# A two-layer hybrid trunk on one core: bias rows from one stacked tile, a third step ahead of the transposes, and the end of the last quad after the first output product

## The chip, the cores and the metric

The kernel runs on one core of one Trainium2 chip. Its time is device microseconds (us) of that core. Three runs of the kernel before took 1513.29 to 1514.67 us, with a median of 1514.11. The engines are named as in the profile: PE (TensorE matmuls), PEld (its weight loads), DVE (VectorE), ACT (ScalarE), POOL (GpSimd), SP (which issues the DMAs).

## The reference

The input has 512 positions of width 1024; 16 learned meta positions are put in front, so that 528 are computed. Layer 0 mixes by two kinds of attention side by side, layer 1 by retention; each is followed by a residual with layer norm and by an MLP with squared ReLU (1024 to 4096 to 1024), a residual and a layer norm. What the change touches:

```python
proj = h @ w_in                      # qa, ka, va | qb, kb, vb | fb
log_f = log_sigmoid(fb + f_bias)     # 8 heads of forgetting attention
cum_f = cumsum(log_f, axis=1)        # along the positions
# differential attention: 4 heads, two softmaxes each, chunk mask
p_diff = p_a[:, :, 0] - lam * p_a[:, :, 1]
# forgetting attention: 8 heads, causal
s_b = (qb . kb) * scale_b + cum_f[q] - cum_f[k]
o_b = softmax(where(frame_vis, s_b, -inf)) @ vb
# MLP
y = square(relu(h @ w1)) @ w2
```

## The kernel before

Positions lie along the free axis: an activation is eight tiles of 128 features by 528 positions, worked on as two halves of 264. Products run in fp32r, with each operand split into a high and a low part; a product is three matmuls (high by high, high by low, low by high). The high part of a weight tile is cast by ACT (`wh`, L228), the low part comes from DVE (`wl`, L229). Activations are split in the same way (`s`, L352 to L362). All matmuls go through one helper (L156) and all transposes on PE through another (L159), so that rows of the profile with those lines are told apart by their tiles.

Order: instructions are written in program order and a scheduler places them on each engine's queue. For PE the written order is fixed. Pieces of work that do not depend on each other are interleaved by Python generators: a filler yields after each piece, and the attention code calls `next(filler, None)` where PE would otherwise run ahead of ACT and DVE. One piece of a projection is 12 matmuls of 264 columns (`mm`). PSUM is shared: `two_banks` tiles (`mm`, `rows_ps` and the like) come from a ring of two, so that a new one needs the older one's reader to have finished.

Layer 0, in the order of time. The value projection (`v_ps`, 512 columns) comes first. Then the four differential heads run: scores (`s_ps`), a clip with its minimum on DVE (L548), exponentials on ACT (L554), normalization on DVE and ACT (L621 to L625), transposes on PE (`t_ps`, 14 of them), their conversion (`turned`, L583 on ACT and L584 on DVE; `s`, L352 and L353), and the products with the values (`o_ps`). Between them the projections of the next heads run as filler.

During the second differential head the filler also builds the bias of the forgetting heads. `forget_sums` (L489 to L511) makes the cumulative sum of log-forget, 8 rows of 528, and splits it. `forget_rows` (L513 to L530) spreads it over tables: for each pair of heads g and each side (query, key) a tile of 128 rows by 528, whose rows 64 (h % 2) to 64 (h % 2) + 3 hold the sum with its sign in two parts, or ones, so that a matmul of two such tables adds cum_f[q] - cum_f[k] to the scores. A constant selection matrix `sel` (8 rows by 3 x 1024) puts each row in its place: three matmuls of 8 contraction rows for each half of a table (high, low, ones), with PE reading `selr`, the cast of `sel`. Each table is copied to SBUF by ACT (`rows`, L527). The generator yields after both sides of a pair: four steps of two tables.

Then come the four pairs of forgetting heads (`fox_scores`, L738 to L757): four score tiles with one filler step each, one more filler step, the last normalization (`finish(3)`), the small scores of the meta positions (`sm_ps`), then the first head's transposes, a filler step, the second head's transposes, more filler steps, and the products with the values.

The MLP (L1198 on) makes the hidden units in part by Strassen-like quads (`quad_up`, L1148 to L1196): seven products on quarters, `qa` to `qd`, whose last, "22", is held back in `finish`: 12 matmuls into `qc`, an addition on DVE (`up`, L1190), relu and two squares on ACT (L1192 to L1194) and a subtraction on DVE (`g`, L1195). `between()` calls a held-back finish once. Hidden units are worked off in four groups; in the last, the output products of the first two output tiles are taken together, over the hidden tiles 0 to 5 and then over 6 and 7, which the last quad makes. The output products of the others follow in `tail`, together with the residual's layer norm (`bank`).

Of the kernel before, what the change touches and what calls it, by code (L numbers as in the profile page):

```python
# [8 lines left out]
F32 = mybir.dt.float32  # L9
F32R = mybir.dt.float32r  # L10
# [4 lines left out]
P = 128  # L15
# [5 lines left out]
HALF = L // 2  # L21
STACK = 6 * META
# [3 lines left out]
FOX_HEADS = 8  # L26
# [95 lines left out]
def kernel(  # L122
# [20 lines left out]
    act, dve = nc.scalar, nc.vector  # L143
# [16 lines left out]
    pe = Ordered()  # L160
# [13 lines left out]
    def two(dt=F32, name="u"):  # L174
        t = both(dt, name)
        return t[:, 0, :], t[:, 1, :]

    def flat(dt, name):
        return both(dt, name).rearrange("p a b -> p (a b)")[:, :1024]
# [7 lines left out]
    def two_banks(name="mm"):  # L187
        return ps_mm.tile([P, 2, 512], F32, tag="mm", name=name)
# [4 lines left out]
    def f(t):  # L193
        return t.bitcast(F32)
# [85 lines left out]
    def product(outs, pairs, lo=0, hi=None):  # L280
        hi = len(pairs) if hi is None else hi
        for k in range(lo, hi):
            lhs, rhs = pairs[k]
            for i, (a, b) in enumerate(PASSES):
                for dst, sel in outs:
                    pe.matmul(dst, lhsT=lhs[a], rhs=sel(rhs[b]), start=k == 0 and i == 0,
                              stop=k == len(pairs) - 1 and i == 2)
# [61 lines left out]
    def split(src, dst=None, rows=slice(0, P), n=L):  # L349
        src = src[:, :n]  # L350
        h, l = dst or two(F32R, "s")
        act.copy(out=h[rows, :n], in_=src)  # L352
        dve.tensor_tensor(out=l[rows, :n], in0=src, in1=f(h)[rows, :n], op=ALU.subtract)  # L353
        return h, l
# [14 lines left out]
    def load(out, in_):  # L369
        dma = nc.sync.dma_start(out=out, in_=in_)  # L370
        if loads["last"] is not None:
            after(dma, loads["last"])
        loads["last"] = dma
        return dma

    prepare(load)
    for j in range(KT // 2):
# [3 lines left out]
        for i in range(2):  # L381
# [3 lines left out]
                     in_=f(pair)[:, :, :META].rearrange("p a (o n) -> p a o n", o=1).broadcast_to([P, 2, 2, META]))  # L385
# [3 lines left out]
    lv_sb, b4_sb = two(F32, "lv_b4")  # L389
    lv_sb = lv_sb[:, :256].rearrange("p (a b) -> p a b", a=4)  # L390
    b4_sb = b4_sb[:, :512].rearrange("p (a b) -> p a b", a=4)
    sel = [flat(F32, "sel") for _ in range(3)]
    nb = two(F32, "nb") + two(F32, "nb")
    fm = two(F32, "fm")[0]
    dve.memset(ones, 1.0)
# [2 lines left out]
    def load_constants():  # L398
        for h in range(DIFF_HEADS):
            load(out=nb[h], in_=c_nb[h])  # L400
        load(out=mb_sb, in_=c_mb)
        load(out=lv_sb, in_=lamv)
        load(out=ident, in_=c_id)
        load(out=wfb_sb, in_=wfb)
        load(out=fb_sb, in_=fbias)
        for j in range(3):
            load(out=sel[j][0:FOX_HEADS], in_=c_sel[j])
        load(out=fm, in_=c_fm)
        load(out=e4_sb, in_=c_e4[:, :4 * PAIR].rearrange("p (a b) -> p a b", a=4))
        load(out=b4_sb[:PAIR], in_=c_e4[:PAIR, 4 * PAIR:].rearrange("p (a b) -> p a b", a=4))  # L410
        load(out=sub_sb, in_=subln)
        load(out=lnp_sb, in_=lnp)
# [64 lines left out]
    R8 = slice(0, FOX_HEADS)  # L477
# [11 lines left out]
    def forget_sums(ze, into):  # L489
        z, e, t, r = (v[R8] for v in ze + two(F32, "ft"))  # L490
        dve.scalar_tensor_tensor(out=e, in0=z, scalar=-1.0, in1=z, op0=ALU.mult, op1=ALU.max)
        act.activation(out=e, in_=e, func=AF.Exp, scale=-1.0)
        yield
        dve.tensor_scalar(out=t, in0=e, scalar1=1.0, scalar2=None, op0=ALU.add)
        dve.tensor_scalar(out=r, in0=t, scalar1=-1.0, scalar2=None, op0=ALU.add)
        dve.tensor_tensor(out=e, in0=e, in1=r, op=ALU.subtract)
        yield
        act.activation(out=t, in_=t, func=AF.Ln)
        act.activation(out=r, in_=t, func=AF.Exp, scale=-1.0)
        dve.tensor_tensor(out=e, in0=e, in1=r, op=ALU.mult)  # L500
        yield
        dve.tensor_tensor(out=t, in0=t, in1=e, op=ALU.add)
        dve.scalar_tensor_tensor(out=z, in0=z, scalar=0.0, in1=t, op0=ALU.min, op1=ALU.subtract)
        yield
        dve.memset(r, 1.0)
        cum = two(F32, "cum")[0][R8]
        dve.tensor_tensor_scan(out=cum, data0=r, data1=z, initial=0.0, op0=ALU.mult, op1=ALU.add)
        one = two(F32R, "one")[0]
        act.copy(out=one[R8], in_=r)
        yield  # L510
        into += [t[R8] for t in split(cum, rows=R8)] + [one[R8]]  # L511

    def forget_rows(srcs, table):  # L513
        selr = [flat(F32R, "selr") for _ in range(3)]
        for j in range(3):
            act.copy(out=selr[j][R8], in_=sel[j][R8])
        yield
        for g in range(4):
            sides = two(F32R, "rows")
            for side in range(2):  # L520
                ps = two_banks("rows_ps")
                for b in range(2):
                    for j in range(3):
                        m = (2 * g + side) * 3 + j
                        pe.matmul(ps[:, b, :HALF], lhsT=selr[m // 8][R8, P * (m % 8):P * (m % 8) + P],
                                  rhs=srcs[j][:, b * HALF:b * HALF + HALF], start=j == 0, stop=j == 2)
                act.copy(out=on(sides[side], FULL), in_=ps[:, :, :HALF])  # L527
                if side:
                    yield
            table.append(sides)  # L530

    MAPS = [slice(64 * m, 64 * m + 64) for m in range(2)]
# [205 lines left out]
    def fox_scores(pair, q, k, filler):  # L738
        pools = [two(F32, "e") for _ in range(3)]
        maps = [key_tiles([t[m] for t in pools]) for m in range(2)]  # L740
        sums = []

        def finish(i):
            for m in range(2):
                r = small([P, 1], "r")
                dve.reciprocal(out=r, in_=sums[i][m])
                dve.tensor_scalar(out=maps[m][i], in0=maps[m][i], scalar1=r, scalar2=None, op0=ALU.mult)

        for i in range(4):
            sums.append(score_tiles(q, k, i, fm, fox_rows[pair], [t[i] for t in maps]))  # L750
            if i:
                finish(i - 1)
            next(filler, None)
        next(filler, None)
        finish(3)
        meta_scores(q, k, fox_rows[pair], 8 + 2 * pair, sm_f)
        return maps  # L757
# [57 lines left out]
    for h in range(4):  # L815
        q, k = got
        got = []
        if h < 3:
            filler = qk_filler(got)
            if h == 0:  # L820
                next(filler)
            if h == 1:
                filler = alternate(filler, forget_sums(fb_ps, sums))
            if h == 2:
                filler = alternate(filler, forget_rows(sums, fox_rows))
        else:
            bw = [weights("B") for _ in range(4)]
            filler = value_filler(bw, vb)
# [369 lines left out]
    def mlp(hs, full, a, b, norm, gs, steps=LN_STEPS):  # L1198
        ts = []
        mix = combined(a, b, ts)  # L1200
        while len(gs) < 8:
            dst = two(F32R, "g")
            get, run = job(hs, squared(dst))
            run(get(), full)
            gs.append(dst)
            for _ in range(4):
                next(mix, None)
        run_all(mix)
        left = {"finish": lambda: None}

        def between():
            left["finish"]()
            left["finish"] = lambda: None

        def quads(into, n):
            for _ in range(n):
                gh, gl = both(F32R, "g"), both(F32R, "g")
                left["finish"] = quad_up(hs, ts, a, b, (gh, gl), between)
                into += [(gh[:, i, :], gl[:, i, :]) for i in range(2)]

        for g in range(NG):
            nxt = []
            if g and g + 1 < NG:
                quads(nxt, 1)
            jobs = [job(gs, add_into(y[k], ALPHA if g == 0 else None)) for k in range(KT)]
            if g + 1 == NG:
                between()
                parts = [dense_parts(weights("A"), gs, full) for _ in range(2)]
                for lo, hi in ((0, 6), (6, 8)):
                    for _, outs, pairs in parts:  # L1230
                        product(outs, pairs, lo, hi)
                for k, (ps, _, _) in enumerate(parts):
                    add_into(y[k], None)(ps, full)
                parts = ps = outs = pairs = None
                pe.on = False
                return tail(jobs[2:], full, a, b, norm, steps)
            for k, (get, run) in enumerate(jobs):
                run(get(), full)
                if k == 0:
                    between()  # L1240
                advance()
                advance()
            pe.on = True
            gs = nxt
            quads(gs, 4 - len(gs) // 2)
# [251 lines left out]
```

## Time and profile before

| what | value |
| --- | --- |
| median of three runs | 1514.11 us |
| the profiled execution | 1510.88 us |
| its span | 1509.1 us |
| PE busy | 1468.2 us, 97% |
| DVE / ACT busy | 889.0 us, 59% / 661.0 us, 44% |
| mean granted PE clock | 0.985 |
| PE waits for ACT's copy of `rows` | 4.1 us in 4 waits |
| first and last start of a `rows_ps` matmul | 92.9 and 120.8 us |

All views are of one profiled execution. A row of the timeline gives start, duration, engine, line, operation and tile, and in brackets the idle time of the engine before it with what released it. Runs of short matmuls stand in one row with their count; the duration of such a row runs to the modelled end of the last, so the spacing of the starts is the rate. A granted clock of 0.5 means that a matmul takes twice the time. The views of windows cut the span at chosen times and give each engine's busy time and the clock in each.

### The profile page before, as it was taken

The numbers are of one execution on the slowest core, as the hardware profiler recorded it, in microseconds if no ns is written. First come the engines' busy times: TensorE is split into PE (matmuls) and PEld (weight loads), VectorE is DVE, ScalarE is ACT, GpSimd is POOL, SyncE is SP. The second block draws the span as 40 slices with busy tenths as digits, with TensorE's granted clock in tenths as the row PEclk, the third lists the DMA queues.
The fourth block names the chain that finished last, engine by engine and source line by source line (L and its number), as shares of the span: only waits on it lengthen the run. The fifth ranks groups of instructions, "written<-read, shape, count | busy, mean of one in ns | idle before, by whom it ended". The sixth has DMA issues, their size and how long they took to land.

```text
span 1509.1 us, 23262 instructions
## 1 busy us (share of the span) xinstructions
PE 1468.2 (97%) x9776; PEld 1329.8 (88%) x9776; DVE 889.0 (59%) x1498; ACT 661.0 (44%) x1024; POOL 0.2 (0%) x4
## 2 busy tenths in 40 slices
PE   8998999999999999999999999999999999999996
PEld 6877888899999999999888888888899889898986
DVE  4553468677747566558534354244378748566567
ACT  4563345536426344255343343153445526444342
POOL 0000000000000000000000000000000000000000
PEclk9987999999999999999999999999999999999998
DMA  7102111240313314243014035023150313314221
GB/s 247 57 29 70 28 43 32 100 165 6 107 56 99 126 59 138 59 145 119 27 42 134 19 110 167 1 72 109 42 182 29 112 48 107 126 56 140 74 81 56
DMA packets 39592, 129.07 MB, mean 86 GB/s; under 512 B 4724, under 2 KB 7172, under 8 KB 39488
## 3 DMA queue, kind: packets, MB, share of 16 engines
q1 hardware_dynamic: 39488, 127.59, 26.3%
q8 instruction: 76, 1.25, 0.3%
q14 instruction: 28, 0.23, 0.1%
HBM read 125.48 MB, written 2.10 MB: 85 GB/s over the span
## 4 chain that ended last, share of the span: by engine, by line
PE 90%; DVE 5%; ACT 3%; DMA 1%; issue 1%; ACTq 0%; DVEq 0%
PE bank L156 35%; PE mm L156 18%; PE v_ps L156 10%; PE qc L156 7%; PE o_ps L156 5%; PE qa L156 4%; PE s_ps L156 3%; PE qb L156 2%; PE qd L156 2%; DMA raw<-in_w 1%; PE t_ps L159 1%; PE sum_ps L156 1%; DVE wl L229 1%; ACT wh L228 1%; DVE y L966 1%
## 5 line engine op out<-in xcount | busy, mean ns | idle before, releaser
L229 DVE TENSOR_TENSOR wl<-raw,wh 128x1024 fp32r<-128x1024 f32 x200 | 242.1, 1220 | 73.3 <-ACT wh L228 72.9
L228 ACT CAST wh<-raw 128x1024 fp32r<-128x1024 f32 x200 | 206.1, 1046 | 112.0 <-DMA raw<-in_w 82.4
L156 PE MATMUL bank<-g,wh 128*128 128x512 f32 (+2 forms) x800 | 201.4, 342 | 1.0 <-ACT wh L228 1.0
L156 PEld LDWEIGHTS bank<-g,wh 128*128 128x128 f32 x800 | 137.3, 188 | 20.1 <-ACT wh L228 2.1
L156 PE MATMUL bank<-hh,wh 128*128 128x512 f32 (+3 forms) x448 | 144.1, 337 | 0.0
L156 PE MATMUL bank<-hh,wl 128*128 128x512 f32 (+3 forms) x448 | 140.3, 329 | 0.0
L156 PE MATMUL bank<-g,wl 128*128 128x512 f32 (+2 forms) x400 | 136.1, 341 | 0.0
L156 PE MATMUL mm<-g,wh 128*128 128x264 f32 x832 | 135.1, 284 | 0.5 <-ACT wh L228 0.5
L156 PE MATMUL bank<-hl,wh 128*128 128x512 f32 (+3 forms) x448 | 120.5, 331 | 4.3 <-DVE hl L958 4.3
L156 PEld LDWEIGHTS mm<-g,wh 128*128 128x128 f32 x832 | 115.3, 188 | 0.7 <-ACT wh L228 0.7
L156 PE MATMUL qc<-tc,wh 128*128 128x264 f32 (+1 forms) x576 | 106.3, 283 | 3.1 <-DVE up L1186 3.1
L156 PE MATMUL mm<-s,wh 128*128 128x264 f32 x544 | 96.8, 302 | 1.2 <-DVE od L727 1.2
L156 PEld LDWEIGHTS bank<-hh,wh 128*128 128x128 f32 x448 | 84.1, 188 | 10.6 <-ACT hh L970 1.2
L156 PEld LDWEIGHTS qc<-tc,wh 128*128 128x128 f32 x576 | 88.8, 188 | 3.7 <-DVE up L1186 3.5
L156 PEld LDWEIGHTS bank<-hh,wl 128*128 128x128 f32 x448 | 84.0, 188 | 8.4
L156 PEld LDWEIGHTS mm<-s,wh 128*128 128x128 f32 x544 | 79.5, 199 | 6.8 <-issue 2.7
L156 PEld LDWEIGHTS bank<-hl,wh 128*128 128x128 f32 x448 | 72.5, 188 | 13.9 <-DVE hl L958 4.9
L156 PE MATMUL mm<-g,wl 128*128 128x264 f32 x416 | 84.6, 285 | 0.0
L156 PEld LDWEIGHTS bank<-g,wl 128*128 128x128 f32 x400 | 75.2, 188 | 9.4 <-DVE wl L229 0.2
L156 PE MATMUL qc<-tc,wl 128*128 128x264 f32 (+1 forms) x288 | 81.7, 284 | 0.0
L228 ACT CAST wh<-sums 128x1024 fp32r<-128x1024 f32 x48 | 50.2, 1046 | 62.8 <-DVE sums L242 40.5
L229 DVE TENSOR_TENSOR wl<-sums,wh 128x1024 fp32r<-128x1024 f32 x48 | 58.6, 1221 | 24.2 <-PE mm L156 10.2
(315 smaller groups left out, 3107.3 us busy)
## 6 DMA issues: line engine op xcount, KB each, us to landing
raw<-in_w SPq DMA_DIRECT2D x224, 512.0 KB, 3.8
xf<-in_x SPq DMA_DIRECT2D x8, 264.0 KB, 5.6
y<-in_x SPq DMA_DIRECT2D x8, 264.0 KB, 4.1
out<-y SPq DMA_DIRECT2D x8, 256.0 KB, 2.2
nb<-in_c_nb SPq DMA_DIRECT2D x4, 264.0 KB
rd<-in_c_rd SPq DMA_DIRECT2D x4, 256.0 KB
rd<-in_c_rm SPq DMA_DIRECT2D x4, 192.0 KB, 4.0
fm<-in_c_fm SPq DMA_DIRECT2D x1, 264.0 KB, 2.7
```

The costliest lines, as they stand in the source:

```text
L156: return self.put(nc.tensor.matmul(*a, **k))
L159: return self.put(nc.tensor.transpose(*a, **k))
L228: act.copy(out=wh, in_=raw)
L229: dve.tensor_tensor(out=wl, in0=raw, in1=f(wh), op=ALU.subtract)
L966: dve.tensor_tensor(out=t, in0=t, in1=r, op=ALU.mult)
```

## The change

Three parts.

Bias rows: the three 8-row selection tiles become one of 96 rows (high rows from 0, low rows from 32, ones from 64), and the three sources become one tile `stack` of 96 rows with the same layout. DVE fills a base tile (64 rows of 0 and 32 of 1), ACT casts it into `stack` and casts the 8 high and the 8 low rows over it. A half of a table is one matmul with 96 contraction rows in place of three with 8. The generator yields after each table: eight steps of one table.

Third step: `fox_scores` takes one more filler step ahead of `finish(3)`. Since the filler has as many pieces as before, one fewer is left for later.

Last quad: `between()` moves from ahead of the two output products of the last group to behind the first of them (the later calls find nothing to do).

```diff
-    sel = [flat(F32, "sel") for _ in range(3)]
+    sel = flat(F32, "sel")
...
-        for j in range(3):
-            load(out=sel[j][0:FOX_HEADS], in_=c_sel[j])
+        load(out=sel[:STACK], in_=c_sel)
...
-        one = two(F32R, "one")[0]
-        act.copy(out=one[R8], in_=r)
-        yield
-        into += [t[R8] for t in split(cum, rows=R8)] + [one[R8]]
+        base, stack = two(F32, "base")[0], two(F32R, "stack")[0]
+        dve.memset(base[:64], 0.0)
+        dve.memset(base[64:STACK], 1.0)
+        act.copy(out=stack[:STACK], in_=base[:STACK])
+        h, l = split(cum, rows=R8)
+        yield
+        act.copy(out=stack[R8], in_=f(h)[R8])
+        act.copy(out=stack[32:32 + FOX_HEADS], in_=f(l)[R8])
+        into.append(stack[:STACK])
...
-        selr = [flat(F32R, "selr") for _ in range(3)]
-        for j in range(3):
-            act.copy(out=selr[j][R8], in_=sel[j][R8])
+        selr = flat(F32R, "selr")[:STACK]
+        act.copy(out=selr, in_=sel[:STACK])
         yield
         for g in range(4):
             sides = two(F32R, "rows")
             for side in range(2):
                 ps = two_banks("rows_ps")
+                m = 2 * g + side
                 for b in range(2):
-                    for j in range(3):
-                        m = (2 * g + side) * 3 + j
-                        pe.matmul(ps[:, b, :HALF], lhsT=selr[m // 8][R8, P * (m % 8):P * (m % 8) + P],
-                                  rhs=srcs[j][:, b * HALF:b * HALF + HALF], start=j == 0, stop=j == 2)
+                    pe.matmul(ps[:, b, :HALF], lhsT=selr[:, P * m:P * m + P],
+                              rhs=srcs[0][:, b * HALF:b * HALF + HALF], start=True, stop=True)
                 act.copy(out=on(sides[side], FULL), in_=ps[:, :, :HALF])
-                if side:
-                    yield
+                yield
             table.append(sides)
...
             next(filler, None)
+        next(filler, None)
         next(filler, None)
         finish(3)
...
             if g + 1 == NG:
-                between()
                 parts = [dense_parts(weights("A"), gs, full) for _ in range(2)]
                 for lo, hi in ((0, 6), (6, 8)):
                     for _, outs, pairs in parts:
                         product(outs, pairs, lo, hi)
+                        between()
```

The host's constant `c_sel` is laid out to match (96 rows by 1024).

On PE, at the tables before, around the second pair of them (`o_ps` is the product of differential head 1 with the values, `mm` a projection's piece):

```order
L156 MATMUL mm<-s,wl 128x264 x2
L156 MATMUL rows_ps<-s,selr 128x264 [waits Activation_49]
L156 MATMUL rows_ps<-s,selr 128x264
L156 MATMUL rows_ps<-one,selr 128x264
L156 MATMUL rows_ps<-s,selr 128x264 x2
L156 MATMUL rows_ps<-one,selr 128x264
L156 MATMUL rows_ps<-s,selr 128x264 [waits Activation_49]
L156 MATMUL rows_ps<-s,selr 128x264
L156 MATMUL rows_ps<-one,selr 128x264
L156 MATMUL rows_ps<-s,selr 128x264 x2
L156 MATMUL rows_ps<-one,selr 128x264
L156 MATMUL s_ps<-s 128x264 [waits DVE_49]
```

In the changed kernel, from the second table to the fourth on PE:

```order
L156 MATMUL rows_ps<-stack,selr 128x264 [waits Activation_49]
L156 MATMUL rows_ps<-stack,selr 128x264
L156 MATMUL s_ps<-s 128x264 [waits DVE_49]
...
L156 MATMUL mm<-s,wl 128x264 x2
L156 MATMUL rows_ps<-stack,selr 128x264 [waits Activation_49]
L156 MATMUL rows_ps<-stack,selr 128x264
L156 MATMUL mm<-s,wh 128x264 [waits Activation_49]
L156 MATMUL mm<-s,wh 128x264 x3
L156 MATMUL mm<-s,wl 128x264 x2
L156 MATMUL mm<-s,wh 128x264 x4
L156 MATMUL mm<-s,wl 128x264 x2
L156 MATMUL rows_ps<-stack,selr 128x264 [waits DVE_49]
```

Where two tables of six matmuls stood in a row there is one of two, and the next stands behind a piece of work; the first `mm` behind the third table, the start of the K projection, now waits for ACT.

On PE, in the first pair of forgetting heads (the first four rows are one projection piece ahead of the meta scores `sm_ps`; `t_ps` are the transposes):

```order
+L156 MATMUL mm<-s,wh 128x264 x4
+L156 MATMUL mm<-s,wl 128x264 x2
+L156 MATMUL mm<-s,wh 128x264 x4
+L156 MATMUL mm<-s,wl 128x264 x2
 L156 MATMUL sm_ps<-s 16x16 x6
 L156 MATMUL sm_ps<-rows 16x16 x2
...
 L159 MATMUL t_ps<-ident,e 128x128 x10
 L159 MATMUL t_ps<-ident,e 16x128 x4
-L156 MATMUL mm<-s,wh 128x264 x4
-L156 MATMUL mm<-s,wl 128x264 x2
-L156 MATMUL mm<-s,wh 128x264 x4
-L156 MATMUL mm<-s,wl 128x264 x2
```

Twelve matmuls have moved from behind the second transposes to ahead of the meta scores; the other pairs read alike.

On PE, at the last quad of layer 0's MLP in the changed kernel (the first `qc` run is an earlier product of that quad, the second its "22"; `mm<-g` are the two output products):

```order
L156 MATMUL qc<-tc,wl 128x264
L156 MATMUL mm<-g,wh 128x264 x4
...
L156 MATMUL mm<-g,wl 128x264 x2
L156 MATMUL qc<-tc,wh 128x264 [waits DVE_49]
L156 MATMUL qc<-tc,wh 128x264
L156 MATMUL qc<-tc,wl 128x264
...
L156 MATMUL qc<-tc,wl 128x264
L156 MATMUL mm<-g,wh 128x264 [waits Activation_49]
L156 MATMUL mm<-g,wh 128x264 x3
L156 MATMUL mm<-g,wl 128x264 [waits DVE_49]
```

Before, the two `qc` runs followed each other directly, and both output products came behind them. In the changed kernel the 36 matmuls of the first output product stand between.

More of the change, by code (lines that the diff above doesn't have):

```diff
@@ L1452 @@
     c_mb[:, 8:] = np.where(mj > mi, BIG, 0.0)[:, None, :]
-    c_sel = np.zeros((FOX_HEADS, 4, 2, 3, P))
+    c_sel = np.zeros((3, 32, 4, 2, P))
     for h in range(FOX_HEADS):
         g, base = h // 2, 64 * (h % 2)
-        c_sel[h, g, 0, 0, base] = -1.0
-        c_sel[h, g, 0, 1, base + 1] = -1.0
-        c_sel[0, g, 0, 2, base + 2:base + 4] = 1.0
-        c_sel[0, g, 1, 2, base:base + 2] = 1.0
-        c_sel[h, g, 1, 0, base + 2] = 1.0
-        c_sel[h, g, 1, 1, base + 3] = 1.0
+        c_sel[0, h, g, 0, base] = -1.0
+        c_sel[1, h, g, 0, base + 1] = -1.0
+        c_sel[2, 0, g, 0, base + 2:base + 4] = 1.0
+        c_sel[2, 0, g, 1, base:base + 2] = 1.0
+        c_sel[0, h, g, 1, base + 2] = 1.0
+        c_sel[1, h, g, 1, base + 3] = 1.0
     c_e4 = np.zeros((P, 4 * PAIR + 4 * P))
@@ L1481 @@
         "c_mb": c_mb.astype(f32),
-        "c_sel": c_sel.reshape(FOX_HEADS, 3, 1024).transpose(1, 0, 2).astype(f32),
+        "c_sel": c_sel.reshape(STACK, 1024).astype(f32),
         "c_e4": c_e4.astype(f32),
```

## The prediction

> **What bounds the kernel now.** I read the page's busy times and slices first, then its chain of waits.
>
> ```profile
> PE 1468.2 (97%) x9776; PEld 1329.8 (88%) x9776; DVE 889.0 (59%) x1498; ACT 661.0 (44%) x1024; POOL 0.2 (0%) x4
> ...
> PEclk9987999999999999999999999999999999999998
> ...
> PE 90%; DVE 5%; ACT 3%; DMA 1%; issue 1%; ACTq 0%; DVEq 0%
> ```
>
> TensorE (PE) is busy for 97% of the span and carries 90% of the chain. A change can gain only where PE idles, does needless work, or runs at a reduced clock; the clock row dips in the third and fourth slice (75 to 151 us), where the bias tables are built. Next, what PE waited for (total, times, longest):
>
> ```profile
> PE rows_ps L156 <- ACT rows L527: 4.1, 4, 1.9
> PE v_ps L156 <- DVE s L353: 3.2, 1, 3.2
> PE qc L156 <- DVE up L1186: 3.1, 2, 1.6
> PE t_ps L159 <- DVE s L362: 2.6, 2, 1.9
> PE bank L156 <- ACT wh L228: 1.0, 3, 0.6
> PE t_ps L159 <- DVE e L747: 0.7, 1, 0.7
> PE t_ps L159 <- DVE turned L584: 0.6, 2, 0.3
> PE mm L156 <- ACT wh L228: 0.5, 1, 0.5
> ```
>
> The first row is the tables' own wait, the t_ps rows lie in the forgetting attention's turns, the qc and wh rows around the MLP's last quad. Each part of the change aims at one of these groups. Last, the stretch of the tables, cut where the granted clock changed (in each row: window, its length, busy time and count of PE, PEld, DVE, ACT, POOL, then the clock):
>
> ```profile
> 94.34:97.75 3.41, 1.93 (x11) 1.66 (x12) 0.37 (x1) 2.35 (x7) 0.00 (x0) 1.00 0.30 118
> 97.75:104.60 6.85, 6.85 (x27) 5.51 (x26) 1.35 (x7) 1.97 (x6) 0.00 (x0) 0.50 0.00 0
> 104.60:108.00 3.40, 2.71 (x21) 2.22 (x21) 0.50 (x1) 1.17 (x3) 0.00 (x0) 1.00 0.00 0
> 108.00:111.35 3.35, 3.35 (x22) 3.11 (x19) 1.92 (x12) 2.00 (x6) 0.00 (x0) 0.50 0.00 0
> 111.35:114.60 3.25, 2.46 (x17) 1.96 (x16) 2.48 (x7) 3.11 (x6) 0.00 (x0) 0.99 0.00 0
> 114.60:125.00 10.40, 9.71 (x41) 8.93 (x42) 1.09 (x1) 1.77 (x3) 0.00 (x0) 0.51 0.18 52
> ...
> 230.55:234.10 3.55, 3.04 (x15) 2.74 (x15) 3.43 (x10) 1.63 (x4) 0.00 (x0) 0.55 0.19 18
> ```
>
> Each time PE idles 0.7 to 1.5 us of a window of about 3.4 us here, the next window runs at half clock. (Not without exception: PE was 0.76 us idle in
>
> ```profile
> 254.40:257.90 3.50, 2.74 (x24) 2.24 (x20) 3.50 (x13) 1.73 (x3) 0.00 (x0) 1.00 0.01 2
> ```
>
> and stayed at full rate after it.) That makes 6.85 + 3.35 + 10.40 = 20.6 us at half clock between 97.75 and 125; half of it, 10.3 us, is lost, less 0.3 for the idle time inside. I take 10.0. This is more than the waits themselves.
>
> **Part 1, the bias rows.**
>
> ```profile
> L156 PE MATMUL rows_ps<-s,selr x32: 276/286/584, 92.9 to 120.5; 8*128 8x264 f32 x32
> L156 PE MATMUL rows_ps<-one,selr x16: 273/278/420, 93.3 to 120.8; 8*128 8x264 f32 x16
> L527 ACT CAST rows<-rows_ps x8: 571/598/601, 95.2 to 121.2; 128x528 fp32r<-128x528 f32 x8
> ```
>
> 48 matmuls become 16. The pitch comes from two rows of PE's timeline, six full-clock matmuls apart and of the same 264 columns:
>
> ```profile
> 656.21 0.65 PE L156 MATMUL mm<-g,wh 128*128 128x264 f32 x4
> ...
> 656.94 0.65 PE L156 MATMUL mm<-g,wh 128*128 128x264 f32 x4
> ```
>
> 0.73 / 6 = 0.122 us each, so 32 removed are worth 3.9 us. One table per step removes the cause of the 4.1 us wait: two tables in a row share PSUM banks with the projection, so that the second had to await the copy (0.6 us) of the one before. It gains 4.1. With both gone I expect the half clock to go too: 10.0. The wait at the end of the stretch stays,
>
> ```profile
> 133.02 1.22 PE L156 MATMUL v_ps<-wh,s 128*128 128x512 f32 x2 [3.17 <-DVE s L353]
> ```
>
> since the transposes' conversion on VectorE follows directly; a stretch with less VectorE work left over might shorten it to 2.8, so 0.4. Gains at full clock: 3.9 + 4.1 + 10.0 + 0.4 = 18.4.
>
> Against this stand new waits. The stack is built ahead of the first table: two memsets on VectorE, the cast of a 96x528 base, and two 8x528 casts on ScalarE in place of one; of the three selr casts two go:
>
> ```profile
> 77.76 0.50 DVE L505 MEMSET ft<- 8x528 f32 x1
> ...
> 91.34 2.93 ACT L516 CAST selr<-sel 8x1024 fp32r<-8x1024 f32 x3
> ```
>
> Two memsets at 0.5 (528 columns as well) and a cast at 0.6 by the rows copy make 1.6 us. They sit in the queues of VectorE and ScalarE before the last exponent products (e, 128x528) of differential head 1, whose transposes PE already awaits:
>
> ```profile
> 87.14 1.42 PE L159 MATMUL t_ps<-ident,e 128*128 128x128 f32 x11 [0.53 <-DVE e L625]
> ```
>
> All of it goes on the path, and its scores behind then wait for the conversion another 0.75 by my walk through the new order. The removed 1.95 us of selr casts come too late to repay this, since by then PE waits for scores, not for selr. The bounds: 0 (the adds stay hidden) and 3.4 (they show twice). Further on, the third table (the order puts it ahead of the K projection's first matmul, which waits for its copy) is copied only after two exponents and a projection copy on ScalarE. The walk puts the table's end at about 103 and the copy's at 104.95, 1.95 us of wait; bounds 0 and 3. The last two tables still stand in a row, and the eighth waits for the seventh's copy: 0.95 us with its latency, as 0.69 and 0.79 in the old pairs; bounds 0.6 and 1.2. The load of 393 KB where three of 32 KB were lies near 35 us, with no PE wait on it between 40 and 70: nothing.
>
> Sum at full clock: 18.4 - 1.6 - 0.75 - 1.95 - 0.95 = 13.2 us. The 1.95 us wait is of the size that cost the clock before (1.48 us idle in 94.34:97.75). One such window costs half of 3.4, 1.7 us; at a chance of three in four I take 1.3 off: 11.9.
>
> The Trainium skill, page "TensorE: Matmul & The Clock Gate", Part 1, says that the gate knows only half and full rate, looks at free-running windows of about 3.4 us, falls after a window that was idle, and returns after about 3.4 us of sustained work. The trace agrees on half and full and on the grid. It disagrees on the rest: a window with PE busy 2.71 of 3.40 us was followed by half rate, and 6.85 us of unbroken work passed before full rate came back. By the page's rule no drop follows the new 1.95 us wait, and the sum would be 13.2 here and 1492.9 in all; I go by the rows.
>
> **Part 2, the third step.** Twelve matmuls, 1.46 us, move from behind the second turn to ahead of the first transposes, in four pairs of heads.
>
> ```profile
> 199.95 1.75 PE L159 MATMUL t_ps<-ident,e 128*128 128x128 f32 x14 [0.69 <-DVE s L362]
> ...
> 203.40 1.75 PE L159 MATMUL t_ps<-ident,e 128*128 128x128 f32 x14 [0.24 <-DVE turned L584]
> ...
> 231.06 3.25 PE L159 MATMUL t_ps<-ident,e 128*128 128x128 f32 x14 [1.92 <-DVE s L362]
> ...
> 288.12 1.09 PE L159 MATMUL t_ps<-ident,e 128*128 128x128 f32 x8 [0.65 <-DVE e L747]
> ```
>
> Pair 0 gains 0.69 and pair 3 0.65. Pair 1 gains 1.46 of its 1.92 and, since only 0.46 us of idle remains in that window, probably the half clock behind it (1.7, of which about 0.5 returns as a turned wait like pair 0's 0.24, which the half clock had hidden; I count 0.8). Pair 2 has no wait ahead of its first transposes and gains nothing. Sum 3.6; bounds 2.8 (the clock stays) and 4.9 (also the turned waits go). What lost its cover is the attention product behind the second turn: twelve matmuls fewer stand ahead of it. Its first half needs the first turn's tiles, which are long done, so I cost that at nothing; if it did wait, 1 us per pair.
>
> **Part 3, the last quad.**
>
> ```profile
> 654.65 0.51 PE L156 MATMUL qc<-tc,wh 128*128 128x264 f32 x2 [1.53 <-DVE up L1186]
> ...
> 661.25 0.75 PE L156 MATMUL mm<-g,wh 128*128 128x264 f32 x4 [0.47 <-ACT wh L228]
> ...
> 662.20 0.51 PE L156 MATMUL bank<-g,wh 128*128 128x264 f32 x2 [0.20 <-ACT wh L228]
> ```
>
> The quad's last twelve products wait until VectorE has emptied their bank, and the next weights' casts stand on ScalarE behind the quad's square. With one output product (36 matmuls, 4.4 us) moved between, the bank is long empty, and the new order has the three weight casts ahead of the relu. Gained: 1.53 + 0.47 + 0.20 = 2.2 in layer 0, and by the waits above (3.1 and 1.0 + 0.5 in all) 2.4 in layer 1: 4.6. The quad's result g is late next: from the last qc matmul to its end pass 656.3 to
>
> ```profile
> 660.30 1.26 DVE L1195 TENSOR_TENSOR g<-up,g 128x1056 fp32r<-128x1056 f32 x1 [3.46 <-ACT up L1194]
> ```
>
> 661.56, 5.3 us, and only the last quarter of the products reads it. The second product (4.4 us) and some two dozen bank matmuls (2.9 us) stand ahead of that: covered by 2 us. I take 4.4 for both; bounds 0 (g's chain is stretched by the casts on VectorE) and 4.6.
>
> **The sum**: 11.9 + 3.6 + 4.4 = 19.9 us. The profiled execution took 1510.88 us around a span of 1509.1, so 1491.0; it lay 3.2 us under the median of the runs, which gives 1494.2, forecast **1494**.
>
> **Rivals.** (1) The half clock stays: PE still idles in three places of the stretch, and if as much time as before (20.6 us) runs slow, 10.3 are lost instead of 1.3; gain 10.9, time 1503. For it speaks that every window there with 0.69 us of idle or more led to a slow one; against, that fewer such windows are left. (2) Neither new table wait appears (1.95 + 0.95), nor the clock drop: gain 24.1, and with all turns covered 25.4, time 1489. For it: ScalarE is busy for only 12.4 of the 30.7 us of the six windows from 94.34 on; against: the copies' order is fixed. (3) The quad's move swaps one wait for another: g arrives late and part 3 is worth nothing; 1498.6. For it, the 5.3 us of latency; against, 7.3 us of cover. (4) Slower: the clock falls at the new waits near 88 us and is not regained until the value products at 138. The full-clock gain of all parts is 13.2 + 3.6 + 4.4 = 21.2 us, and each microsecond at half rate costs 0.5, so this decides from 42 us of half clock. From 88 to 138 there are 50 us: 25 lost, 3.8 slower, 1518. For it, 97.75 to 125 held only two short full-rate windows; against, that the clock did return there while PE still idled, and with 20.6 us. By the return rule of the Trainium skill's page "TensorE: Matmul & The Clock Gate", Part 1, this one could not happen.
>
> **How the numbers follow.** The forecast has 0.53; rival 1 0.18, rival 2 0.14, rival 3 0.11, rival 4 0.04. The forecast's own spread is 1490 to 1499 (bounds of the new waits). To hold eight in ten the range takes rival 3 whole, most of rival 1 and half of rival 2: **1488 to 1503**. A difference of 0.2%, about 3 us, is what a measurement of this kernel can tell. Only rival 4 ends slower (0.04); a mix of rivals 1 and 3 with all costs at their upper bounds could end within 0.2%: 0.03, taken from rival 1; faster 0.93.
>
> **What would show it.** Right: rows_ps waits near 1 us in all, and PE's clock at 1.0 in most windows from 95 to 120; the t_ps waits on L362's line down from 2.6 to 0.5; the qc wait and the wh waits of mm and bank gone in both layers. Wrong: half clock for more than 10 us between 95 and 120; a transpose wait at 87 us that grew by far more or less than 1.6; the mm or bank matmuls of the last quarter waiting for g.

## The result and the profile after

The changed kernel takes 1486.41 us (median of 4 runs, 1484.54 to 1490.04) against 1513.7 (4 runs, 1511.94 to 1514.67): a ratio of 0.9824, 95% interval 0.9802 to 0.9845, so 27 us faster. The forecast was 1494 with a range from 1488 to 1503: the direction was right, the gain was a third larger than forecast, and the time lies just below the range.

Page of the changed kernel: engines, the granted clock by slice, the chain.

```profile
PE 1454.1 (98%) x9744; PEld 1320.3 (89%) x9744; DVE 889.9 (60%) x1500; ACT 659.3 (44%) x1024; POOL 0.2 (0%) x4
...
PEclk9989999999999999999999999999999999999998
...
PE 92%; DVE 5%; ACT 2%; issue 1%; DMA 0%; ACTq 0%
```

PE runs 32 matmuls fewer, and the dip in the third and fourth slice has shrunk to one slice. PE's waits in the changed kernel (total, times, longest):

```profile
PE v_ps L156 <- DVE s L353: 2.3, 1, 2.3
PE mm L156 <- ACT rows L529: 2.0, 1, 2.0
PE t_ps L159 <- DVE e L626: 1.8, 1, 1.8
PE t_ps L159 <- DVE turned L585: 1.3, 3, 0.8
...
PE rows_ps L156 <- ACT rows L529: 0.9, 1, 0.9
PE t_ps L159 <- DVE s L362: 0.5, 1, 0.5
PE o_ps L156 <- DVE s L353: 0.3, 1, 0.3
PE mt_ps L159 <- DVE s L353: 0.3, 1, 0.3
```

The qc wait and the waits for wh are gone. The two forecast waits at the tables are there nearly to the digit (1.99 and 0.94, forecast 1.95 and 0.95). The transposes' wait came too, but smaller than forecast (1.80 instead of 0.53, so 1.27 more, forecast 1.6). The stretch of the tables, cut where the clock changed (columns as in the prediction):

```profile
85.60:88.95 3.35, 1.85 (x18) 1.25 (x16) 3.32 (x11) 2.92 (x6) 0.00 (x0) 1.00 0.28 114
88.95:95.75 6.80, 6.40 (x31) 5.38 (x31) 4.08 (x9) 5.08 (x10) 0.00 (x0) 0.50 0.00 0
95.75:106.00 10.25, 10.25 (x79) 8.96 (x80) 4.56 (x23) 4.94 (x14) 0.00 (x0) 1.00 0.18 54
106.00:109.40 3.40, 1.41 (x11) 1.20 (x11) 1.61 (x10) 3.40 (x8) 0.00 (x0) 1.00 0.00 0
109.40:112.75 3.35, 3.35 (x18) 3.35 (x17) 2.44 (x3) 1.72 (x3) 0.00 (x0) 0.51 0.25 65
112.75:119.60 6.85, 5.91 (x52) 5.52 (x52) 1.57 (x4) 3.92 (x7) 0.00 (x0) 0.99 0.12 47
119.60:123.10 3.50, 1.28 (x14) 0.85 (x12) 3.28 (x5) 3.33 (x5) 0.00 (x0) 1.00 0.45 139
123.10:126.50 3.40, 3.35 (x8) 2.68 (x9) 3.38 (x7) 1.22 (x2) 0.00 (x0) 0.50 0.74 189
```

In this execution half clock follows the 1.80 us wait and the 1.99 us wait; the 0.94 us wait (before 118.03, in the sixth row) is followed by full rate, and the wait at the value products, in the row after that, by half rate again.

The two profiled executions took 1510.88 and 1490.04 us, 20.8 apart: the forecast sum of 19.9 looks right there. The medians are 27 apart, so that agreement is luck. Each run also has its span and mean clock, and these explain it: a run's time falls into span x clock (time at full rate) and span x (1 - clock), the clock loss (what half rate cost; 4 to 5 us of it lie at the end of every profiled span, where PE has no work left). The clock is recorded to 0.001, which is 1.5 us of a span, so the values of single runs are that coarse. The profiled execution of the changed kernel, clock 0.990, lost 14.9 us; its other three runs 7.4, 10.4 and 10.4.

| kernel | runs | median us | ratio to before (95%) | span x clock, mean | clock loss, mean (range) |
| --- | --- | --- | --- | --- | --- |
| before | 67 | 1513.0 | | 1487.4 | 23.6 (18 to 30) |
| changed | 8 | 1486.3 | 0.9824 (0.981 to 0.9838) | 1474.8 | 10.4 (7.4 to 14.9) |
| rows alone | 4 | 1495.4 | 0.9878 (0.9863 to 0.9893) | 1482.6 | 10.8 (9.0 to 11.9) |
| third step alone | 12 | 1510.8 | 0.998 (0.9967 to 0.9993) | 1485.9 | 22.8 (20 to 27) |
| quad alone | 8 | 1506.6 | 0.9958 (0.9939 to 0.9976) | 1478.8 | 26.2 (23 to 30) |
| third step and quad | 5 | 1502.6 | 0.9925 (0.9911 to 0.9939) | 1478.4 | 22.2 (18 to 24) |

Of the 26.7 us, 12.7 are in span x clock and 13.2 in the clock (medians and means are mixed here, hence the small rest). The ratio in the second row is that of the second set of runs; the first set's is the same with a wider interval.

### The profile page after: what moved, and what is told of

It reads as the page before. It is cut to its first block, busy times and chain, and to the rows that moved or that the text cites. A ratio compares the mean times of both kernels' runs of the same rounds, so it can differ in the third digit from the quotient of the medians.

```text
span 1488.2 us, 23198 instructions
## 1 busy us (share of the span) xinstructions
PE 1454.1 (98%) x9744; PEld 1320.3 (89%) x9744; DVE 889.9 (60%) x1500; ACT 659.3 (44%) x1024; POOL 0.2 (0%) x4
## 4 chain that ended last, share of the span: by engine, by line
PE 92%; DVE 5%; ACT 2%; issue 1%; DMA 0%; ACTq 0%
PE bank L156 37%; PE mm L156 19%; PE v_ps L156 11%; PE qc L156 7%; PE o_ps L156 5%; PE qa L156 4%; PE s_ps L156 3%; PE qd L156 2%; PE qb L156 2%; PE t_ps L159 1%; DVE wl L229 1%; PE sum_ps L156 1%; DVE y L968 1%; DVE e L549 0%; ACT wh L228 0%
## 5 line engine op out<-in xcount | busy, mean ns | idle before, releaser
L156 PE MATMUL mm<-s,wh 128*128 128x264 f32 x544 | 93.8, 295 | 3.1 <-ACT rows L529 2.0
L156 PEld LDWEIGHTS bank<-hh,wh 128*128 128x128 f32 x448 | 84.9, 190 | 10.4 <-ACT hh L972 1.2
```

The source lines that it names most:

```text
L156: return self.put(nc.tensor.matmul(*a, **k))
```

## The experiments

**The kernels again.** No edit.

> The kernel before once more, to see the clock of each run. The two profiled runs, before and changed, differ by 20.8 us (forecast 19.9), the medians by 27.3. Theory W (a run's time is one fixed amount of full-clock time plus half of whatever time the throttle grants at half clock): span times mean granted clock is the same in every run, 1486.5 +- 1.5 us as in the profiled run (1509.1 x 0.985), and the clocks lie near 0.983, a little under the profiled 0.985, where the time is higher. Theory V (the 3 us by which the profiled run lay under the median are work or transfers, not clock): clocks all 0.985, and span times clock rises with the time to 1489 and more.

Measured: 1511.37 us, ratio 0.9991 (0.9981 to 1.0001). Over its 11 runs span x clock lies between 1486.9 and 1489.3, the clock between 0.983 and 0.987; the time follows the clock (0.987: 1509.0 to 1510.7; 0.983: 1514.35). Theory W holds in the main: the clock moves with the time, though span x clock lies up to 1.3 us above its band.

> The changed kernel once more. Theory W: span times clock 1474 +- 1.5 us in every run (1488.2 x 0.990 = 1473.3 in the profiled one), clocks between 0.989 and 0.996, times 1484 to 1491 with the lowest at the highest clock; median near 1487. Theory V: the spread of 5.5 us is not matched by the clock, span times clock varies by over 4 us.

Measured: 1486.29 us, ratio 0.9824 (0.981 to 0.9838); clocks 0.994, 0.994, 0.995 and 0.990, the last in the slowest run (1490.41). Span x clock is 1473.7 to 1476.3, up to 0.8 us above the band. Theory W holds in the main; the profiled execution of the changed kernel was one of its slower ones.

**One part alone.** The rows' hunks, with the third step and the quad as before:

> The bias rows alone, without the third step and the moved quad. By the traces of before and after, the changed kernel was 10.9 us ahead behind the tables' stretch (at the next differential head's value product). Theory W: 9 to 16 us faster than before, ratio 0.989 to 0.994, of it about 4 in span times clock (32 matmuls 3.9; the old table waits of 4.1 against new ones of about as much) and the rest in the clock, 0.985 to 0.990. Rival P (the prediction's term, 11.9, is right and the surplus of the whole lies in the other two parts): 11 to 13 us. Rival N: 18 us or more, so that the surplus of the whole is here.

Measured: ratio 0.9878, 18.5 us (16 to 21). Span x clock 4.9 lower, clock loss 12.8 lower. That is Rival N by the median, with an interval that reaches down to Theory W's 16: most of the surplus of the whole is here, and it is in the clock.

The other two parts without the rows:

> The third step and the moved quad without the bias rows. The prediction gave 3.6 + 4.4 = 8.0 us. By the traces of before and after the stretch of the four pairs gained 4.3 and the two quads with what follows them 4.2 and 3.6, 12.1 together. Theory W: 10 to 13 us faster, nearly all of it in span times clock, the clock at 0.984 to 0.986. Rival P: 8 us. Rival N (the surplus needs all parts together): 5 us or less.

Measured: ratio 0.9925, 11.3 us (9 to 13), 9.1 of it in span x clock. More than the forecast 8.0, as Theory W said. The two gains add up to 29.8, 3 more than the whole gained; their intervals are wide enough for that. Each alone:

```diff
+        next(filler, None)
         next(filler, None)
         finish(3)
```

> The third step alone. The prediction gave 3.6 us, of it 2.8 in waits ahead of the transposes (0.69 + 1.46 + 0.65) and 0.8 in the clock. Third step and quad together took 9.1 us off span times clock (1487.5 to 1478.4). Theory W: span times clock 1484.0 to 1485.2 (2.3 to 3.5 less), clock as before or one window better, time 2 to 5 us lower, ratio 0.9967 to 0.9987. Rival Q (the surplus of the two parts lies here, not in the quads): span times clock down by 4.7 or more.

Measured: ratio 0.998 (0.9967 to 0.9993), 3.0 us; span x clock 1.5 lower, less than either theory had. The trace of the changed kernel shows where the rest went (timeline of PE, pairs 1 and 3):

```profile
217.88 1.75 PE L159 MATMUL t_ps<-ident,e 128*128 128x128 f32 x14 [0.46 <-DVE s L362]
...
221.86 0.33 PE L159 MATMUL t_ps<-ident,e 128*128 128x128 f32 x1 [0.78 <-DVE turned L585]
...
278.19 0.25 PE L159 MATMUL mt_ps<-ident,sm_f 16*16 16x16 f32 x4 [0.31 <-DVE s L353]
...
278.79 0.96 PE L156 MATMUL o_ps<-s 128*128 128x512 f32 x3 [0.34 <-DVE s L353]
```

In pair 1 the wait ahead of the first transposes fell from 1.92 to the expected 0.46, and 0.78 of it came back ahead of the second, which wait for the first ones' conversion. In pair 3 the wait of 0.65 went, and two new ones came: the 12 matmuls had been all that stood between the second transposes and the products that need them.

The quad alone:

```diff
-                between()
                 parts = ...
                 for lo, hi in ((0, 6), (6, 8)):
                     for _, outs, pairs in parts:
                         product(outs, pairs, lo, hi)
+                        between()
```

> The moved quad alone. The prediction gave 4.4 us, the waits that vanish (2.2 + 2.4). Theory W, from the sum of 9.1 less the third step's 2.8: span times clock down by 6 to 6.6, so that the move saves more than the waits it removes, partly where the layer norm follows; clock unchanged; ratio 0.995 to 0.9965. Rival Q: 4.4 us, and the surplus lies in the third step.

Measured: ratio 0.9958 (0.9939 to 0.9976), 6.4 us; span x clock 8.6 lower, and a clock loss 2.5 higher than before in its 8 runs, which no part of the edit explains (the ranges overlap). So the surplus over 4.4 is here. Its place is seen by setting PE's starts against the pitch of full-rate matmuls (0.122 us for 264 columns, 0.118 for 256, 0.231 for 512). From the first matmul of the `qc` product ahead of the last quad's "22" to the layer norm's first sum PE took 38.8 us before and 35.0 in the changed kernel in layer 0 (651.49 to 690.31, 636.49 to 671.53), and 25.9 and 22.4 in layer 1 (1441.28 to 1467.18, 1423.43 to 1445.88). That is 7.2 us, where the waits in brackets made 4.6; 0.4 of it is a wait ahead of layer 0's sum, which the 4.6 did not count. The first wait, in the kernel before:

```profile
652.83 0.28 PE L156 MATMUL qc<-tc,wl 128*128 128x264 f32 x1
654.65 0.51 PE L156 MATMUL qc<-tc,wh 128*128 128x264 f32 x2 [1.53 <-DVE up L1186]
655.00 0.28 PE L156 MATMUL qc<-tc,wl 128*128 128x264 f32 x1
```

The bracket counts from the modelled end of the matmul before, 653.11, but by the pitch the next would have started at 652.95: the starts lose 1.70 where the bracket has 1.53, and the second matmul behind the wait is 0.11 late as well. Around the wait of 0.20 before 662.20 they lose 0.46, and 0.30 and 0.11 more follow.

**The new waits.** Filling them with needless work of PE:

```diff
+                    for _ in range(12 if m == 2 and b else 0):
+                        pe.matmul(...)     # the same matmul again
...
-                pe.transpose(...)
+                for _ in range(1 + (extra if c == 2 and blocks is banks[0] else 0)):
+                    pe.transpose(...)      # extra = 12 for head 1
```

> The changed kernel with needless work of PE put into two of its waits: 12 repeated transposes in front of the one that waits 1.80 us, and 12 repeated matmuls of the third table, behind which 1.99 us were waited for its copy (each some 1.46 us; the results are the same, since they write the same values again). Theory H (idle time of PE inside a window makes the throttle halve the next one): with the waits down to some 0.4 and 0.6 us, the half-clock windows that followed them (6.7 us from 89.0, 3.1 us from 109.5) are gone from the profile, span times clock stays within 1.5 us of 1474.8 and the time falls by 1 to 4 us although PE does more, ratio to the kernel before 0.979 to 0.982. Rival K (it is the kind of work around the wait, transposes and small matmuls, or the place in the program, not the idle time): half-clock windows at both places as before, time the same or higher by up to 1 us.

Measured: ratio 0.9821 (0.9799 to 0.9843), the same time; the waits fell to 0.5 and 0.8. The profiled execution has no half clock between 85 and 118, where the changed kernel's first profile had 10 us of it and its second 3.4, but over five runs the clock loss is 9.2 against 10.4 with ranges that overlap. The forecast gain of 1 to 4 us isn't there; the cost of these two waits in the clock stays unsettled by this pair.

Making the base early:

```diff
     def forget_sums(ze, into):
+        base, stack = two(F32, "base")[0], two(F32R, "stack")[0]
+        dve.memset(base[:64], 0.0)
+        dve.memset(base[64:STACK], 1.0)
+        act.copy(out=stack[:STACK], in_=base[:STACK])
...
-        (the same four lines behind the scan)
```

> The changed kernel with the two memsets and the base's cast at the start of the forget sums, a differential head earlier, instead of ahead of the last exponent product. Theory W: the transposes' wait of 1.80 us falls to 0.5 to 0.9 (0.53 before the change), span times clock by 0.7 to 1.5, and the half clock from 89.0 mostly goes: time 1 to 4 us under the changed kernel, ratio 0.979 to 0.982. Rival S (not the memsets but the order behind the two casts of the sum's split holds the product up): the wait stays at 1.3 or more and the time within 1 us of the changed kernel.

Measured: 1484.64 us, ratio 0.9806 (0.9783 to 0.9829). The 1.80 us wait is gone (0.8 us in two waits), span x clock 2.1 lower, clock loss 10.0. Theory W for the wait. The half clock behind it is gone from the profile (none between 85 and 106 us), but the mean clock loss did not fall.

**What makes the half clock.** The rows' part has two halves: fewer, taller matmuls, and one table per step. Each alone:

```diff
-                if side:
-                    yield
+                yield
```

> The kernel before with one edit: a step after each table instead of after two (still three 8-row matmuls per half, 48 in all). The bias rows alone took 4.9 us off span times clock and 13 us of the loss to half clock. Theory G (the pairing makes the waits, and the waits the half clock): the waits for the rows copy fall from 4.1 to 2 to 3, the clock loss (span times one minus clock) falls from 24 to 10 to 15 us, span times clock by 0 to 2 us since the 32 matmuls stay; ratio 0.990 to 0.994. Rival M (matmuls of 8 rows hardly count as work for the throttle, so half clock comes with them, waits or not): clock loss 19 to 24 as before, ratio 0.997 to 1.001.

Measured: ratio 0.9945 (0.9927 to 0.9963), clock loss 15.8 (12 to 23), span x clock 1485.4. The wait for the rows copy fell to 0.7, with one of 1.1 for VectorE's split ahead of a projection's piece. A clock loss of 15.8 lies between the two theories, next to Theory G's 10 to 15, so neither alone.

```diff
-                yield
+                if side:
+                    yield
```

(in the rows' part, so 96 rows and two tables per step)

> The bias rows alone, but with two tables per step as before (16 matmuls of 96 rows, in four pairs). Theory G: each second table waits for the copy of the first, some 0.6 to 0.9 us longer ahead than before since fewer matmuls stand between (waits for the rows copy 4 to 6 us), the half clock comes back at least in part: clock loss 17 to 24, span times clock 1482 to 1485; ratio 0.993 to 0.999. Rival M: clock loss 10 to 13 as with one table per step, ratio 0.987 to 0.991.

Measured: ratio 0.9938 (0.9923 to 0.9953), clock loss 15.5 (12 to 23), span x clock 1485.3: again between the two theories. PE waited longer ahead of the tables than before the change (3.1 us for copies and 2.4 us for a split, against 4.1), and still lost 8 us less to the clock. Waits alone cannot be the cause. The last run keeps the pairs and the 48 matmuls and changes their rows, with the stack that this needs:

```diff
+                    for _ in range(3):
                         pe.matmul(...)     # 96 rows
```

> Two tables per step and 48 matmuls for them, as in the kernel before, but each of 96 rows: the one matmul of a half is written three times over (the same values again). One table per step with 8 rows brought the clock loss from 23.5 to 15.8 us, two per step with 16 matmuls of 96 rows to 15.5 although PE waited longer for the copies (5.5 us in all against 4.1). Rival M (a stretch of 8-row matmuls counts to the throttle like idle time, 1.5 us for twelve of them): the clock loss is 12 to 17 us here too, although waits and number of matmuls are as before; span times clock 1486 to 1489; ratio 0.993 to 0.997. Theory G (only waits and pairing count; what helped with 16 matmuls was their smaller number, which moves the work against the throttle's windows): clock loss 20 to 24 us, ratio 0.998 to 1.002.

Measured: ratio 0.9949 (0.9931 to 0.9967), clock loss 15.3 (10.5 to 18; the kernel before, run beside it, 25.0), span x clock 1488.7. That is Rival M. Its waits for the rows copy, 3.7 us in four, are close to the 4.1 of before. In its profile two windows of the tables read:

```profile
96.20:99.60 3.40, 2.71 (x21) 2.46 (x20) 0.94 (x6) 2.15 (x7) 0.00 (x0) 1.00 0.49 157
99.60:103.00 3.40, 3.40 (x22) 2.58 (x21) 0.09 (x1) 1.03 (x2) 0.00 (x0) 1.00 0.00 0
103.00:106.40 3.40, 2.71 (x21) 2.50 (x21) 1.76 (x8) 2.35 (x6) 0.00 (x0) 1.00 0.00 0
106.40:109.90 3.50, 3.50 (x34) 3.21 (x33) 1.89 (x11) 1.72 (x4) 0.00 (x0) 1.00 0.00 0
```

PE busy 2.71 of 3.40 us in 21 matmuls, twice, and full rate after it (in the clock's own windows, 0.2 us later, 2.73 and 2.72). The prediction showed the window 104.60:108.00 of the kernel before: also 2.71 of 3.40 us busy, also 21 matmuls, twelve of them of 8 rows, and half rate after it. What differs is the rows.

The profile before shows the same from the other side. Two of its drops follow windows without any wait:

```profile
183.09:186.50 3.41, 3.41 (x31) 3.18 (x29) 0.45 (x1) 0.93 (x4) 0.00 (x0) 1.00 0.00 0
186.50:189.91 3.41, 3.41 (x18) 3.04 (x18) 3.01 (x7) 2.30 (x6) 0.00 (x0) 0.50 0.15 14
...
299.14:302.55 3.41, 3.41 (x27) 3.24 (x27) 3.35 (x4) 2.27 (x4) 0.00 (x0) 1.00 0.41 117
302.55:305.97 3.42, 3.42 (x18) 3.42 (x17) 2.00 (x4) 1.49 (x3) 0.00 (x0) 0.50 0.99 331
```

Twelve matmuls in each of the two full-rate windows have 16 rows and 16 columns (`mo_ps`). An estimate over all 15 profiles: count each matmul as 0.44 ns per column (the pitches of 512 and 256 columns differ by 0.113 us) times its rows over 128, in the 6228 full-rate windows of 3.41 us on the clock's own grid (without the first 20 us and the time after 1460 us). Of 36 windows that were filled to less than 0.30 by this count 34 were followed by half rate, of 52 between 0.30 and 0.40 again 34, and of 6140 above that 1. Without the weight by rows, 33 of these 69 drops follow windows filled to over 0.45. This is a count over traces and not an experiment.

**Better versions.** With the early base, the third step in the first three pairs only:

> The kernel with the early base, and the third step in the first three pairs only. In the fourth the step took away the 12 matmuls between the second transposes and the meta transposes, which then waited (0.31 and 0.34 us, 1.4 us more than the pitch of their matmuls) against 0.65 us (1.0) saved. Expected: those two waits gone, the one of 0.65 back, span times clock 1472.0 to 1473.5 (1472.7 with the step in all four), ratio 0.979 to 0.982. Rival: the fourth pair's step was worth something, span times clock 1473.5 or more.

Measured: 1484.85 us, ratio 0.982 (0.9806 to 0.9835), span x clock 1472.6: no difference from the step in all four. The 0.65 us wait is back, the two others gone; the fourth pair's step was worth nothing. And with two tables copied by VectorE:

```diff
-                act.copy(out=on(sides[side], FULL), in_=ps[:, :, :HALF])
+                (dve.tensor_copy if m in (2, 6) else act.copy)(out=on(sides[side], FULL), in_=ps[:, :, :HALF])
```

> As the run with the third step in three pairs, and the third and the seventh table copied by VectorE, which idles there, in place of ScalarE, where the third copy stood behind two exponentials. Theory W: the wait of the K projection's first matmul falls from 1.99 to 0.8 to 1.2, that of the eighth table from 0.94 to 0.5 to 0.8; span times clock 1471 to 1472.5, half clock around 106 rarer; ratio 0.977 to 0.981. Rival: a fresh copy on VectorE delays the exponent products, the same time or slower.

PE's waits in it, the two that belong to the tables:

```profile
PE mm L156 <- DVE rows L529: 0.8, 1, 0.8
PE rows_ps L156 <- DVE rows L529: 0.8, 1, 0.8
```

Measured: 1482.81 us (1481.24 to 1483.82), ratio 0.9807 (0.9793 to 0.9821), span x clock 1470.5, 4.3 below the changed kernel. This is the fastest version run. Its interval overlaps the changed kernel's.

## Why the prediction was right and wrong

**Part 1, forecast 11.9 us, measured 18.5 (16 to 21).** The full-rate terms were about right: forecast 3.2 (13.2 less the 10.0 of clock), measured 4.9. By its own terms: the 3.9 for 32 matmuls and the 4.1 of old waits stand, the new waits came at 1.27, 1.99 and 0.94 (forecast 1.6, 1.95, 0.95), the further 0.75 of scores behind the transposes did not appear, and the wait at the value products fell by 0.9 (3.17 to 2.27) instead of 0.4; together 4.7.

The step that failed is the clock term, 10.0 less 1.3, so 8.7; measured 12.8. Two things were wrong in it. First, its size: 10.0 counted the half clock between 97.75 and 125 alone and took the half clock from 131.89 to 138.71, two windows, and what lies behind it for fixed. In the profiled execution of the changed kernel this pair became one window (123.10 to 126.50, 1.7 us lost instead of 3.4). Where the runs without a profile saved their clock is not shown. Second, its mechanism: "Each time PE idles 0.7 to 1.5 us of a window of about 3.4 us here, the next window runs at half clock." The three windows of the tables that were read this way held short waits together with six to twelve 8-row matmuls. With 96 rows in those matmuls waits of 0.69 us led to no half clock, twice, in the three-fold run's profile (the one of 1.61 us did). The exception that the prediction noted, 254.40:257.90 with 0.76 us idle and full rate behind, was the hint: it holds no 8-row matmuls. The two drops behind windows without a wait (at 186.50 and 302.55) it did not look at. The taller matmuls alone lower the clock loss by 8 us, one table per step alone by 7.8, both together by 12.8; the prediction valued the former only at their 3.9 us of work.

The drop behind the 1.99 us wait, put at a chance of three in four, is seen in one of the two profiles of the changed kernel, and the one behind the 1.80 us wait, which was not forecast, in both.

**Part 2, forecast 3.6, measured 3.0 (1.1 to 5.0).** The size is right by luck. The waits of pairs 0 and 1 went as worked out, and the half clock at 230.87 is gone from the profile of the third step alone; the turned wait in pair 1 came back at 0.78 (0.5 forecast). The step "what lost its cover ... I cost that at nothing" failed in pair 3, where 12 matmuls were the whole cover; the bound of 1 us per pair given beside it was nearer there (two waits, 0.65 together).

**Part 3, forecast 4.4, measured 6.4 (3.6 to 9.2), by the traces 7.2.** The mechanism is right: the three waits vanish in each layer, and g is not waited for. The sum was undersized since it added the idle times in brackets. A wait cost PE more than its bracket: the stretches shrank by 7.2 us where brackets made 4.6, since a bracket starts only at the modelled end of the matmul before and the matmuls behind a wait are late as well (0.11 us in the first case).

**The sum** of 19.9 was set against the profiled execution and then carried to the median with the same offset of 3.2 us. In full-rate time the whole gained 12.7 (forecast 10.4: 3.2 + 2.8 + 4.4), in the clock 13.2 (forecast 9.5: 8.7, and 0.8 in part 2). Rival 2, at 1489, came nearest in time, for the wrong reason: neither of the waits that it left out was absent. Rivals 1, 3 and 4 fell: the clock did not stay low, g came in time.

The Trainium skill's page "TensorE: Matmul & The Clock Gate", Part 1, says that the gate's windows run free, so that what falls into one changes from run to run. The runs agree: with span x clock between 1484 and 1491 us, the loss of the kernel before ranges from 18 to 30 us. Its rule that the rate falls after an idle window is too narrow here: the window 104.60:108.00 was 80% busy.

**What stays open.** How much the two new waits cost in the clock: filling them cleared the profile and not the mean of the runs. And how the throttle weighs a matmul by its rows: only 8 against 96 was run, and the count over the traces has no sharp border between 0.30 and 0.40. Why one table per step alone also lowered the clock loss by 7.8 us is argued from its shorter waits and not tested apart from them.

## What to carry to other kernels

Where the granted clock moves, split each run's time into span x clock and span x (1 - clock) before comparing; a single profiled execution can lie 3 to 4 us off the median through the clock alone. Matmuls that use a few rows of the array can cost more than their time: here, beside short waits, they brought the half clock, so stack the operands to fill the contraction. And to price a wait on the engine that bounds the kernel, set starts against the pitch over the stretch; the bracketed idle time alone is too little.

## What the hardware showed unexpectedly

A window of about 3.4 us with PE busy for 2.71 us led to half rate when twelve of its 21 matmuls had 8 contraction rows, and to full rate when they had 96 (twice in one profile). Over whole runs, raising the rows from 8 to 96 in 48 matmuls, with their number and the waits kept, lowered the loss to half clock from 23.6 to 15.3 us and the time by 7.7 (ratio 0.9949, 0.9931 to 0.9967), though it added the base's memsets and casts.
